# A two-layer decoder trunk: the last 512 columns of the first FFN's shift and scale move behind the layer norm

## The chip, the cores and the metric

The kernel runs on one core of one Trainium2 chip, as one program with one launch. The metric is the device time in microseconds (us); lower is better. A run of this kernel is quoted as the median of several executions. One execution was profiled by the hardware.

The core's engines run side by side and each takes its instructions in order. TensorE (PE, with its weight loads as PEld) multiplies matrices and writes to PSUM, of which this kernel uses eight banks. VectorE (DVE) and ScalarE (ACT) do element-wise work. GpSimd (POOL) does little here. SyncE (SP) issues the DMA loads.

## The reference

The input is one sequence of 256 positions with 2048 channels (`x`), and one conditioning vector `c` of 2048 numbers. There are two layers. Each has a token mixer and a gated FFN with a short convolution, and each of these is wrapped the same way:

```
c_act = silu(c)
for i in 0, 1:
    sh1, sc1, g1, sh2, sc2, g2 = split(c_act @ ada_w[i] + ada_b[i], 6)     # each 2048 long
    h = x * (1 + sc1) + sh1
    y = fox_attention(h)  (layer 0)   or   swa_attention(h)  (layer 1)
    x = layer_norm(alpha * x + (1 + g1) * y)
    h = x * (1 + sc2) + sh2
    u = causal depthwise conv of width 3 over positions of (h @ w_up)      # 2 * 5632 columns
    y = (silu(u[:5632]) * u[5632:]) @ w_down
    x = layer_norm(alpha * x + (1 + g2) * y)
```

All weights are 32-bit floats and stay in main memory until used. Layer 0's `w_up` is 2048 x 11264. `ada_w` is 2048 x 12288 for each layer, so 100 MB a layer for one vector times a matrix.

## The kernel before, in words

**Tiling.** The 2048 channels are 16 chunks of 128. Weights are streamed in blocks of two chunks by 512 columns (`stream`, L258): one DMA of 512 KB into a tile `w` (or, for the conditioning, `wa`) of a pool with ten buffers shared by all loads. Each block is split into a rounded high part `wh` (ScalarE, L266) and a residual `wl` (VectorE, L277), so that three fast matmul passes (high x high, low x high, high x low) give nearly full precision. The modulated activations are held as `hH` and `hL` in the same way. `w_mm` (L311) does one pair of chunks of a 512-column block with the weights stationary: 24 matmuls of 128x256. `x_mm` (L287) does it with the activations stationary: 12 matmuls of 128x512.

**Order.** `stream` does not run matmuls at once. It puts a function for each pair of chunks into the list `work`, and `settle` (L223) runs them two pairs behind. Just before a pair runs, `rest` (L229) issues the VectorE residuals for it and the next two pairs. A function added with `alone=True` (the set `lone`) is not looked past: no residual of a later pair is issued before it has run. The layer norm's function `between` (L1116) is added like that. Each pair calls `run_post` (one step of each deferred evacuation), then the matmuls, then one entry of `feeds` (modulation of two further chunks), then `tick`.

**Conditioning.** `tick` (L357) calls `ada_tick` (L463), which adds `ada["rate"]` to a debt and takes one step of the conditioning generator for each whole unit. `ada_list` (L365) gives the order of the vectors (layer, index): shift and scale of the FFN are 3 and 4, the gates 2 and 5, the mixer's shift and scale 0 and 1. A vector takes 32 steps of one load and one VectorE multiply-add into `acc` (L395, one 128x1024 piece for each of 16 chunks and two halves). A shift or scale vector (a column) is then summed over partitions: four groups of four transposes on TensorE (L433), four ScalarE activations each with a running sum into `tot` (L437), one VectorE addition of the bias (L419). A gate (a row) starts with a bias load by GpSimd and ends with four matmuls and activations (L405 to L407). After vector 4 the generator holds (`ada["held"]`, L442) until the norm has used it. `ada_need` (L469) takes steps until a given vector is there. `rate` is set by stage: 1.6 in the last part of the opening, 1.6, 1.6, 1.5 and 1.4 in the four FoX blocks (the first of these has no pair left by then), 1.3 in layer 0's output projection, 0.64 in its FFN's up-projection, 0.78 in its down-projection, 0.3 and 0.9 in layer 1's attention, 0.4 in its FFN.

**The norm and the FFN.** `residual` (L611) adds the output projection to `x` and gathers statistics. `between` asks for shift and scale in full, merges them with the norm's gain and bias into `G` and `B` (`merged`, L666), and calls `modulate` (L506): eight feeds, each two chunks. A feed normalises 512 columns of `x` where needed (L637 on ScalarE, L639 on VectorE), transposes four 128x128 blocks (L484), and writes `hH` and `hL` (L494 to L496 for the first two pairs, L498, L499, L84 and L85 for the others). Two feeds are run at once, and each further one after a pair of matmuls. `affine` (L650) applies the norm's gain and bias to `x` itself: 16 VectorE instructions (L657, L658) in eight later steps, with four loaded tiles.

`conv_ffn` (L1049) has two parts of 6 and 5 blocks. Each block has a gate column block and a value column block of `w_up` (512 columns each, eight pairs of chunks, two PSUM banks), so part one has 12 column blocks, 96 pairs. `evac` (L1063) takes a finished column block through the convolution, one 128x256 tile every two steps (ScalarE L1056, VectorE L1057 and L1059), then SiLU (L1075) or the gating product (L1080, L84, L85). Then comes the down-projection of that part, which needs gate (0,5).

The program's lists fix the order in which the work is written. A scheduler then places each instruction on its engine; it may move one ahead of others where its inputs and buffers are free, except those marked with `pin`, which keep their order.

Of the kernel before, what the change touches and what calls it, by code (L numbers as in the profile page):

```python
# [17 lines left out]
P = 128  # L18
# [23 lines left out]
def hybrid_trunk(ctx: ExitStack, tc: tile.TileContext, a: dict, out: bass.AP):  # L42
# [13 lines left out]
    def wtile(name="w"):  # L56
        return wp.tile([P, 2, WB], F32, tag="w", name=name)
# [310 lines left out]
    held = []  # L368
    HELD = {}

    def ada_vector(l, v):
        row = v % 3 == 2
        if (l, v) in HELD and HELD[l, v]:
            q = [cst.tile([P, 512], F32, tag=f"ha{i}", name="ha") for i in range(4)]
            part = lambda c, n: q[c // 512][:, c % 512:c % 512 + n]
            step_ = 512
        else:
            acc = cst.tile([P, D], F32, tag="acc", name="acc")
            part = lambda c, n: acc[:, c:c + n]
            step_ = D // 2  # L380
        if row:

            nc.gpsimd.dma_start(acc, a["ada_b"][l, v * D:(v + 1) * D].partition_broadcast(P))
            yield
            yield
        for k in range(KC):
            for c in range(0, D, D // 2):
                w = wtile("wa").rearrange("p a f -> p (a f)")
                pin(nc.sync.dma_start(w, a["ada_w"][l, k * P:(k + 1) * P, v * D + c:v * D + c + D // 2]), False)
                for o in range(0, D // 2, step_):  # L390
                    ac, wo = part(c + o, step_), w[:, o:o + step_]
                    if k == 0 and not row:
                        pin(nc.vector.tensor_scalar_mul(ac, wo, cact[:, 0:1]), True)
                    else:
                        pin(nc.vector.scalar_tensor_tensor(ac, wo, (cactp if row else cact)[:, k:k + 1], ac,  # L395
                                                           op0=ALU.mult, op1=ALU.add), True)
                yield
        if row:
            while not ada["gate_free"]:
                yield  # L400
            ada["gate_free"] = False
            g = cst.tile([P, D], F32, tag="gate", name="gate")
            for j in range(D // 512):
                ps = bank()
                mm(ps, onep, acc[:, j * 512:(j + 1) * 512], start=True, stop=True)  # L405
                yield
                nc.scalar.activation(g[:, j * 512:(j + 1) * 512], ps, AF.Copy, bias=1.0)  # L407
            gates[l, v] = g
            return
        ps = []  # L410

        def sums():
            ps.append(bank())
            for k in range(KC):
                pin(mm(ps[0][:, k:k + 1], part(k * P, P), ones[:, 0:1], start=True, stop=True))

        def finish():
            cv = cst.tile([P, KC], F32, tag=f"cv{v}", name="cv")
            pin(nc.vector.scalar_tensor_tensor(cv, ps[0][:, :KC], 1.0 if v % 3 else 0.0,  # L419
                                               acol[:, l, v * KC:(v + 1) * KC], op0=ALU.add, op1=ALU.add), True)  # L420
            cols[l, v] = cv

        if (l, v) in HELD:
            held.append((sums, finish))
            ada["held"] = not HELD[l, v]
            ready_cols.add((l, v))
        else:

            tot = sp.tile([P, KC], F32, tag="tot", bufs=1, name="tot")
            for k in range(0, KC, 4):  # L430
                tb = bank()
                for j in range(4):
                    nc.tensor.transpose(tb[:, j * P:(j + 1) * P], part((k + j) * P, P), ident)  # L433
                yield
                for j in range(4):
                    o = tb[:, j * P:(j + 1) * P]
                    nc.scalar.activation(o, o, AF.Identity, accum_out=tot[:, k + j:k + j + 1])  # L437
            yield
            ps.append(tot)
            finish()  # L440

            ada["held"] = v == 4  # L442

    ready_cols = set()

    def release():

        for s_, _ in held:
            s_()
        for _, f_ in held:  # L450
            f_()
        held.clear()
        ada["held"] = False

    def ada_step():
        if ada["gen"] is None:
# [10 lines left out]
            ada_step()  # L467

    def ada_need(l, v):  # L469
        while (l, v) not in cols and (l, v) not in gates and (l, v) not in ready_cols:  # L470
            ada_step()


# [29 lines left out]
    def hstat(kc, t):  # L503
        return hH[:, kc, t * P:(t + 1) * P], hL[:, kc, t * P:(t + 1) * P]

    def modulate(G, B, norm):  # L506
# [6 lines left out]
        feeds.extend([lambda k=k: feed(k) for k in range(0, KC, 2)])  # L513
        for _ in range(2):
            feeds.pop(0)()

    def opening(plan, proj, prep):

# [48 lines left out]
        for s_, todo in enumerate(todos):  # L567
            n = len(todo)
            if s_ == len(widths):
                then(lambda: ada.update(rate=1.6))  # L570
                for it in todo:
                    proj(*it)
                break
# [92 lines left out]
    def merged(l, v, lng, lnb, ll):  # L666

        sh, sc = cols[l, v], cols[l, v + 1]
        G = sp.tile([P, KC], F32, tag="G", name="G")
        B = sp.tile([P, KC], F32, tag="B", name="B")  # L670
        nc.vector.tensor_tensor(G, sc, lcol[:, lng, ll, :], op=ALU.mult)
        nc.vector.tensor_tensor(B, sc, lcol[:, lnb, ll, :], op=ALU.mult)
        nc.vector.tensor_tensor(B, B, sh, op=ALU.add)
        return G, B


# [50 lines left out]
    def out_proj(oT, full, w_o, l):  # L727
        def stat(kc, t):
            while kc not in full:
                step()  # L730
            return oT[kc][0][:, t * P:(t + 1) * P], oT[kc][1][:, t * P:(t + 1) * P]

        ps = {d: x_banks() for d in range(2)}

        def part(d, ks):
            use = x_mm_end(ps[d], stat, KC, 2) if d == D // WB - 1 else                 lambda kc, h, l_: x_mm(ps[d], kc, h, l_, stat, KC - 1)
            stream(w_o, 0, d * WB, ks, use)

        for i, ks in enumerate((range(0, 8), range(8, 12))):
            then(lambda i=i: ada.update(rate=((1.3, 1.3, 1.3, 1.3), (0.9,) * 4)[l][i]))  # L740
            for d in range(2):
                part(d, list(ks))
        then(lambda: ada_need(l, 2))
        for d in range(D // WB):
            if d < 2:
                part(d, list(range(12, KC)))
            else:
                then(lambda d=d: ada.update(rate=((1.3, 1.3, 1.3, 1.3), (0.9,) * 4)[l][d]))
# [300 lines left out]
    def conv_ffn(l):  # L1049
# [10 lines left out]
                                           op0=ALU.mult, op1=ALU.add)  # L1060
            return u

        def evac(ps, f0, then):  # L1063
            u = None
            for f in range(5):
                v = conv(ps[f // 2][:, f % 2, :], f0 + f) if f < 4 else None
                if u is not None:
                    then(f - 1, u)
                u = v
                yield  # L1070
                yield

        def silu(sil):
            def f_(f, u):
# [11 lines left out]
        sbs = [(0, 6), (6, NB)]  # L1086
        for si, (b0, b1) in enumerate(sbs):
            gT = []
            then(lambda: ada.update(rate=(0.64, 0.4)[l]))
            for b in range(b0, b1):  # L1090
                ps = w_stationary(w_up, b * WB)
                sil = [ttile("sil") for _ in range(2)]
                then(lambda ps=ps, b=b, sil=sil: defer(evac(ps, b * 4, silu(sil))))
                ps = w_stationary(w_up, DFF + b * WB)
                then(lambda ps=ps, b=b, sil=sil, gT=gT: defer(evac(ps, DFF // P + b * 4, gated(sil, gT))))

            def stat(kc, t, gT=gT):
                while kc >= len(gT):
# [3 lines left out]
            def ready(si=si):  # L1102
                if si == 0:
                    drain()
                ada_need(l, 5)
                ada["rate"] = (0.78, 0.4)[l]

            then(ready)
            for d in range(D // WB):
# [6 lines left out]
    def between(l, v, g, b, name, ll):  # L1116

        ada_need(l, v)
        ada_need(l, v + 1)
        release()  # L1120
        modulate(*merged(l, v, g, b, ll), normalise)
        behind[0] = 2
        later([affine(name, ll)])

    for l in range(DEPTH):
        if l > 0:
# [42 lines left out]
```

## Time and profile before

| | us |
|---|---|
| median of 3 runs | 2259.64 |
| lowest and highest | 2258.59, 2263.47 |
| the profiled execution | 2253.72 |
| its span, first to last instruction | 2251.9 |

In the profile's page, the first lines give the busy time of each engine. The digits after them divide the span into 40 equal slices (56 us each) and give the busy share in tenths. "Stretches" are rows of busy time by engine between two times. "Waits" rows say who waited for whom, then the total in us, how often, and the longest. "Groups" rows give line, engine, operation, what is written from what, shapes, how many, then busy us, mean ns of one, and idle time before them with what ended it. "Timeline" rows give start, duration and instruction in order of time.

The mean granted TensorE clock is 0.993. Layer 0's attention fills the time to about 360 us, its output projection the time to 465 us. The norm's first transposes stand at 470.52 us and the FFN's first matmul at 473.01 us.

### The profile page before, as it was taken

The numbers are of one execution on the slowest core, as the hardware profiler recorded it, in microseconds if no ns is written. First come the engines' busy times: TensorE is split into PE (matmuls) and PEld (weight loads), VectorE is DVE, ScalarE is ACT, GpSimd is POOL, SyncE is SP. The second block draws the span as 40 slices with busy tenths as digits, with TensorE's granted clock in tenths as the row PEclk, the third lists the DMA queues.
The fourth block names the chain that finished last, engine by engine and source line by source line (L and its number), as shares of the span: only waits on it lengthen the run. The fifth ranks groups of instructions, "written<-read, shape, count | busy, mean of one in ns | idle before, by whom it ended". The sixth has DMA issues, their size and how long they took to land. (4 is left out here: it accounts for less than half of the span.)

```text
span 2251.9 us, 38292 instructions
## 1 busy us (share of the span) xinstructions
PE 2197.1 (98%) x14853; PEld 2017.8 (90%) x14853; DVE 1794.3 (80%) x2450; ACT 1175.0 (52%) x1897; POOL 22.8 (1%) x53
## 2 busy tenths in 40 slices
PE   6999999999999999999999999999999999999997
PEld 6999888889999888999987788889999888999986
DVE  6989999979978968788788989779787555666756
ACT  3445656555555443655634588755555533454532
POOL 0000000000000000000000000000000000000000
PEclk9999999999999999999999999999999999999999
DMA  9999999969979989789897767658887566666663
GB/s 339 381 360 365 361 345 323 329 202 339 324 240 310 322 285 337 249 302 309 265 313 282 256 231 251 215 162 303 264 265 257 177 193 194 188 188 189 190 193 112
DMA packets 274248, 602.99 MB, mean 268 GB/s; under 512 B 21063, under 2 KB 29961, under 8 KB 273553
## 3 DMA queue, kind: packets, MB, share of 16 engines
q1 hardware_dynamic: 273008, 595.85, 79.3%
q0 software_dynamic: 1056, 4.69, 0.6%
q8 instruction: 116, 1.90, 0.3%
q14 instruction: 68, 0.55, 0.1%
HBM read 598.37 MB, written 2.10 MB: 267 GB/s over the span
## 5 line engine op out<-in xcount | busy, mean ns | idle before, releaser
L266 ACT CAST wh<-w 128x1024 fp32r<-128x1024 f32 x728 | 764.1, 1051 | 836.0 <-PE ws L75 304.6
L277 DVE TENSOR_TENSOR wl<-w,wh 128x1024 fp32r<-128x1024 f32 x728 | 888.1, 1223 | 352.6 <-ACT wh L266 331.8
L75 PE MATMUL ws<-hH,wh 128*128 128x256 f32 x3328 | 935.2, 282 | 4.9 <-ACT hH L84 2.1
L75 PE MATMUL ws<-hH,wl 128*128 128x256 f32 x3328 | 929.7, 281 | 3.2 <-DVE wl L277 3.1
L75 PE MATMUL ws<-hL,wh 128*128 128x256 f32 x3328 | 931.2, 280 | 0.0
L75 PEld LDWEIGHTS ws<-hH,wh 128*128 128x128 f32 x3328 | 628.7, 189 | 9.4 <-ACT hH L84 2.3
L75 PEld LDWEIGHTS ws<-hL,wh 128*128 128x128 f32 x3328 | 629.9, 189 | 2.9 <-issue 1.9
L75 PEld LDWEIGHTS ws<-hH,wl 128*128 128x128 f32 x3328 | 628.0, 189 | 4.7 <-DVE wl L277 4.6
L75 PE MATMUL xs<-wh,gT 128*128 128x512 f32 x1408 | 435.9, 390 | 0.0
L75 PEld LDWEIGHTS xs<-wh,gT 128*128 128x128 f32 x1408 | 264.4, 188 | 54.8
L75 PE MATMUL xs<-wl,gT 128*128 128x512 f32 x704 | 274.1, 389 | 0.0
L395 DVE SCALAR_TENSOR_TENSOR acc<-wa,cact,acc 128x1024 f32<-128x1024 f32 x180 | 228.5, 1277 | 0.3 <-DMA wa<-in_ada_w_dram 0.3
L395 DVE SCALAR_TENSOR_TENSOR acc<-wa,cactp,acc 128x1024 f32<-128x1024 f32 x128 | 162.7, 1279 | 1.0 <-DMA acc<-in_ada_b_dram 1.0
L75 PEld LDWEIGHTS xs<-wl,gT 128*128 128x128 f32 x704 | 132.2, 188 | 27.0
L75 PE MATMUL xs<-wl,hH 128*128 128x512 f32 x352 | 141.0, 401 | 3.1 <-DVE wl L277 3.1
L75 PE MATMUL xs<-wh,hH 128*128 128x512 f32 x352 | 142.0, 409 | 0.3 <-ACT hH L494 0.3
L75 PE MATMUL xs<-wh,hL 128*128 128x512 f32 x352 | 138.7, 397 | 0.0
L1056 ACT ACTIVATE u<-ws,ccol 128x256 f32<-128x256 f32 x176 | 96.5, 561 | 57.6 <-PE ws L75 49.1
L75 PE MATMUL xs<-wh,oT 128*128 128x512 f32 x384 | 125.1, 395 | 0.1
L1057 DVE SCALAR_TENSOR_TENSOR u<-ws,ccol,u 128x255 f32<-128x255 f32 x176 | 82.9, 480 | 19.0 <-ACT u L1056 19.0
L75 PEld LDWEIGHTS xs<-wh,oT 128*128 128x128 f32 x384 | 72.1, 188 | 14.8 <-ACT oT L84 0.5
L1059 DVE SCALAR_TENSOR_TENSOR u<-ws,ccol,u 128x254 f32<-128x254 f32 x176 | 83.6, 480 | 2.1
(218 smaller groups left out, 1597.3 us busy)
## 6 DMA issues: line engine op xcount, KB each, us to landing
w<-in_ffn_w_up_dram SPq DMA_DIRECT2D x352, 512.0 KB, 4.6
wa<-in_ada_w_dram SPq DMA_DIRECT2D x320, 512.0 KB, 5.5
w<-in_ffn_w_down_dram SPq DMA_DIRECT2D x176, 512.0 KB, 5.0
w<-in_fox_w_in_dram SPq DMA_DIRECT2D x96, 512.0 KB, 7.2
wo<-in_ada_w_dram SPq DMA_DIRECT2D x48, 512.0 KB, 8.9
w<-in_swa_w_in_dram SPq DMA_DIRECT2D x40, 512.0 KB, 5.3
w<-in_fox_w_o_dram SPq DMA_DIRECT2D x32, 512.0 KB, 6.0
w<-in_swa_w_o_dram SPq DMA_DIRECT2D x32, 512.0 KB, 5.2
```

The source lines that it names most:

```text
L75: return nc.tensor.matmul(o, lhsT, rhs, start=start, stop=stop, **kw)
L266: pin(nc.scalar.copy(h, w), False)
L277: pin(nc.vector.tensor_tensor(l, w, f32(h), op=ALU.subtract), behind[0] > 0)
L395: pin(nc.vector.scalar_tensor_tensor(ac, wo, (cactp if row else cact)[:, k:k + 1], ac, op0=ALU.mult, op1=ALU.add), True)
L1056: nc.scalar.activation(u, pf, AF.Identity, bias=cw(CW, f), scale=cw(2, f))
L1057: nc.vector.scalar_tensor_tensor(u[:, 1:], pf[:, :S - 1], cw(1, f), u[:, 1:], op0=ALU.mult, op1=ALU.add)
L1059: nc.vector.scalar_tensor_tensor(u[:, 2:], pf[:, :S - 2], cw(0, f), u[:, 2:], op0=ALU.mult, op1=ALU.add)
```

## The change

The first FFN's shift (0,3) and scale (0,4) are split at column 1536 (`LC` = 12 of 16 chunks). Before the norm, the generator computes columns 0 to 1535 of each: for each chunk one 1024-column piece as before, and for each two chunks one load that carries 512 columns of both, with two narrower multiply-adds. A new entry `(0, "late")` stands behind (0,4) in `ada_list`. It loads, for each of the 16 chunks of rows, the last 512 columns of both vectors with one DMA, and does one 1024-wide multiply-add. Two groups of four transposes and two bias additions finish it.

The first three column blocks of that FFN (gate block 0, value block 0, gate block 1) run over chunks 0 to 11 first, 18 pairs with six PSUM banks held. Then a function added with `alone=True` takes whatever is left of the late vector, merges columns 12 to 15 of `G` and `B`, and runs the last two feeds. Then the three column blocks run over chunks 12 to 15, six pairs. Their evacuations go through one chain that takes one tile a pair (`slow=False`). `affine` is put off to this point. The old way of holding vectors (`HELD`, `release`), which was not used, is removed.

The rates change: 1.4 in the last part of the opening, 1.35, 1.3, 1.3 and 1.25 in the FoX blocks, 1.2 in layer 0's output projection, 1.5 during the 18 pairs, 0.5 after them in the first part of the FFN, 0.7 in its second part, 0.8 in its down-projections.

```diff
-    ada_list = [(0, 3), (0, 2), (0, 4), (0, 5), (1, 0), (1, 1), (1, 3), (1, 2), (1, 4), (1, 5)]
+    ada_list = [(0, 3), (0, 2), (0, 4), (0, "late"), (0, 5), (1, 0), (1, 1), (1, 3), (1, 2), (1, 4), (1, 5)]
...
+        n = LC * P if (l, v) in SPLIT else D
...
         for k in range(KC):
-            for c in range(0, D, D // 2):
...
+            for c in range(0, n, D // 2):
+                w = wtile("wa")
+                if c + D // 2 <= n:
+                    w = w.rearrange("p a f -> p (a f)")
+                    pin(nc.sync.dma_start(w, a["ada_w"][l, k * P:(k + 1) * P, v * D + c:v * D + c + D // 2]), False)
+                    mac(acc[:, c:c + D // 2], w, k)
+                elif k % 2 == 0:
+                    pin(nc.sync.dma_start(w, a["ada_w"][l, k * P:(k + 2) * P, v * D + c:v * D + n]
+                                          .rearrange("(k p) f -> p k f", p=P)), False)
+                    for j in range(2):
+                        mac(acc[:, c:n], w[:, j, :], k + j)
+                else:
+                    continue
                 yield
...
+    LATE, LC = "late", KC - 4
+    SPLIT = {(0, 3), (0, 4)}
+
+    def ada_late(l):
+
+        n = KC - LC
+        acc = cst.tile([P, D], F32, tag="acc", name="acc")[:, :2 * n * P].rearrange("p (v f) -> p v f", v=2)
+        for k in range(KC):
+            w = wtile("wa")
+            pin(nc.sync.dma_start(w, a["ada_w"][l, k * P:(k + 1) * P, 3 * D:5 * D]
+                                  .rearrange("p (v f) -> p v f", f=D)[:, :, LC * P:]), False)
+            if k == 0:
+                pin(nc.vector.tensor_scalar_mul(acc, w, cact[:, 0:1]), True)
+            else:
+                pin(nc.vector.scalar_tensor_tensor(acc, w, cact[:, k:k + 1], acc, op0=ALU.mult, op1=ALU.add), True)
+            yield
+        tot = yield from ada_sums([acc[:, v, k * P:(k + 1) * P] for v in range(2) for k in range(n)])
+        for i in range(2):
+            ada_column(cols[l, 3 + i], tot, l, 3 + i, LC, n, i * n)
+        cols[l, LATE] = tot
...
-        for blk, rate in zip((0, 2, 1, 3), (1.6, 1.6, 1.5, 1.4)):
+        for blk, rate in zip((0, 2, 1, 3), (1.35, 1.3, 1.3, 1.25)):
...
+                then(lambda: ada.update(rate=1.5))
+                for i in range(len(first)):
+                    some(i, range(LC))
+                then(lambda: (late[l](), ada.update(rate=0.5)), True)
+                for i in range(len(first)):
+                    some(i, range(LC, KC))
+                    then(lambda i=i: (done.append(i), i or defer(chain())))
...
+        if (l, v) in SPLIT:
+            GB = merged(l, v, g, b, ll, ks=slice(0, LC))
+            modulate(*GB, normalise, (0, LC))
+
+            def more():
+                ada_need(l, LATE)
+                merged(l, v, g, b, ll, GB, slice(LC, KC))
+                modulate(*GB, normalise, (LC, KC))
+                while feeds:
+                    feeds.pop(0)()
+                later([affine(name, ll)])
+
+            late[l] = more
```

`ada_sums` is the old transposing and summing code, and `ada_column` the old bias addition, both for a given range of columns. `chain` evacuates the three first blocks one after the other.

More of the change, by code (lines that the diff above doesn't have):

```diff
@@ L409, in ada_vector @@
             return
[L410 to L421, printed above, removed]
@@ L444, in hybrid_trunk, with ada_sums @@
[L444 to L453, printed above, removed]
+        tot = yield from ada_sums([acc[:, k * P:(k + 1) * P] for k in range(n // P)])
+        cv = cst.tile([P, KC], F32, tag=f"cv{v}", name="cv")
+        ada_column(cv, tot, l, v, 0, n // P)
+        cols[l, v] = cv
+        ada["held"] = v == 4
+    def ada_sums(blocks):
+        tot = sp.tile([P, KC], F32, tag="tot", bufs=1, name="tot")
+        for k in range(0, len(blocks), 4):
+            tb = bank()
+            for j in range(4):
+                nc.tensor.transpose(tb[:, j * P:(j + 1) * P], blocks[k + j], ident)
+            yield
+            for j in range(4):
+                o = tb[:, j * P:(j + 1) * P]
+                nc.scalar.activation(o, o, AF.Identity, accum_out=tot[:, k + j:k + j + 1])
+        yield
+        return tot
@@ L469, in ada_need @@
     def ada_need(l, v):
-        while (l, v) not in cols and (l, v) not in gates and (l, v) not in ready_cols:
+        while (l, v) not in cols and (l, v) not in gates:
             ada_step()
```

125 lines of the change are left out of this document (62 added, 63 removed).

## The prediction

> **What bounds the kernel now.** I read the page first, then the stretches by stage, then who waited for whom in the stage before the first layer norm, then the order of time at that norm. The page's totals and slices:
>
> ```profile
> span 2251.9 us, 38292 instructions
> ...
> PE 2197.1 (98%) x14853; PEld 2017.8 (90%) x14853; DVE 1794.3 (80%) x2450; ACT 1175.0 (52%) x1897; POOL 22.8 (1%) x53
> ...
> PE   6999999999999999999999999999999999999997
> ...
> DVE  6989999979978968788788989779787555666756
> ```
>
> TensorE sets the time, so only stretches where it stops can give or lose anything. The stages around the change, by stretches (us; then busy us of PE, PEld, DVE, ACT, POOL; granted clock; DMA share; GB/s):
>
> ```profile
> 182.00:255.00 73.00, 71.06 (x529) 66.14 (x530) 69.95 (x112) 47.02 (x93) 5.29 (x11) 1.00 0.99 348
> 255.00:320.00 65.00, 63.23 (x442) 58.50 (x441) 59.72 (x78) 36.26 (x76) 0.00 (x0) 1.00 0.98 351
> 320.00:360.00 40.00, 38.20 (x270) 34.14 (x269) 35.12 (x49) 21.25 (x40) 0.00 (x0) 1.00 0.94 339
> 360.00:465.00 105.00, 103.85 (x496) 86.09 (x495) 91.51 (x120) 55.34 (x115) 0.54 (x1) 1.00 0.92 326
> 465.00:480.00 15.00, 11.39 (x68) 9.98 (x67) 13.60 (x27) 9.33 (x14) 1.12 (x2) 0.89 0.09 27
> ...
> 530.00:580.00 50.00, 50.00 (x431) 50.00 (x430) 49.47 (x65) 26.81 (x37) 0.00 (x0) 1.00 0.99 357
> 580.00:743.00 163.00, 163.00 (x1378) 161.08 (x1378) 138.86 (x177) 86.88 (x122) 0.00 (x0) 1.00 0.86 286
> ```
>
> From 182 to 465 us (FoX blocks and output projection) VectorE is busy 69.95 + 59.72 + 35.12 + 91.51 = 256.3 of 283 us, 91%, and the DMA engines 92 to 99%. From 530 to 580 us the first FFN runs with VectorE full (49.47 of 50) and yet TensorE never stops. From 580 to 743 us VectorE has 163 − 139 = 24 us free. What TensorE and its weight loads wait for between 182 and 465 us:
>
> ```profile
> PE xs L75 <- DVE wl L277: 2.6, 3, 1.8
> PE ws L75 <- DVE wl L277: 2.2, 4, 0.8
> PE sm L433 <- DVE acc L395: 1.4, 2, 1.1
> PE ws L75 <- ACT wh L266: 0.7, 1, 0.7
> ```
>
> ```profile
> PEld xs L75 <- DVE wl L277: 3.9, 4, 2.2
> PEld ws L75 <- DVE wl L277: 3.3, 5, 1.0
> ...
> PEld ws L75 <- ACT wh L266: 1.1, 1, 1.1
> ```
>
> Ends of matmuls are modelled, so I take the weight loads' account where there is one: 3.9 + 3.3 for late residuals `wl`, 1.1 for a late `wh`, and 1.4 for the shift-and-scale accumulator `acc`: 9.7 us. That is all that lighter VectorE and DMA work before the norm can give back.
>
> **The change, part by part.** Loads first. Before, vectors (0,3) and (0,4) have 32 loads of 512 KB each; after, 24 each, and 16 late loads carry the last 512 columns of both. 64 either way: no byte is saved, 16 loads (8.4 MB) move past the norm. VectorE's share, with the rows for 1024 and 512 columns (the second row is another instruction of the same operation, standing in for the new narrow one):
>
> ```profile
> L395 DVE SCALAR_TENSOR_TENSOR acc<-wa,cact,acc 128x1024 f32<-128x1024 f32 x56 | 70.2, 1275 | 0.0
> ```
>
> ```profile
> L277 DVE TENSOR_TENSOR wl<-w,wh 128x1024 fp32r<-128x1024 f32 x38 | 46.5, 1226 | 0.3 <-ACT wh L266 0.3
> L395 DVE SCALAR_TENSOR_TENSOR acc<-wa,cactp,acc 128x1024 f32<-128x1024 f32 x21 | 26.8, 1287 | 0.0
> L1057 DVE SCALAR_TENSOR_TENSOR u<-ws,ccol,u 128x255 f32<-128x255 f32 x15 | 7.3, 488 | 0.5 <-ACT u L1056 0.5
> ...
> L658 DVE SCALAR_TENSOR_TENSOR x<-ln,x 128x512 f32<-128x512 f32 x8 | 5.5, 693 | 0.0
> ```
>
> A split vector costs 16 × 1.28 + 16 × 0.69 = 31.5 us in place of 32 × 1.28 = 41.0, so two of them take 19 us from VectorE before the norm; late, 16 × 1.28 = 20.5 us come back.
>
> *Gain before the norm.* VectorE goes from 256.3 to 237 of 283 us, 91% to 84%; DMA falls by 8.4 of some 96 MB (283 us at about 338 GB/s), 9%. The lower rates spread this: 1.6 to 1.3 in the block from 182 us takes 0.3 × 1.28 = 0.4 us from each pair of chunks, less in later ones. If waits go as load over free time, 0.91/0.09 becomes 0.84/0.16 and they halve: 9.7 × 0.48 = 4.7 us. If every one goes, 9.7. The accumulator's 1.4 us may stay, and both resources lighten together; I take **6.5 us**.
>
> Does the work still end before the norm? Counted in steps of the conditioning generator: before, 38 + 39 + 38 = 115, with 107.8 granted by the end of output columns 0 and 1 and 1.3 for each pair in column 2, so it ends in that column's sixth pair. After, 29 + 39 + 29 = 97, with 93.3 granted by then and 1.2 a pair: the fourth. The last column row of before lies 16.5 us ahead of the norm's closing matmuls, so no wait arises there:
>
> ```profile
> 445.78 0.17 DVE L419 SCALAR_TENSOR_TENSOR cv<-tot,acol 128x16 f32<-128x16 f32 x1
> ```
>
> *Start of the FFN.* The norm's own stop and the two fast pairs stay. One pair of chunks is 24 matmuls; 431 in 50 us make 0.116 us each, 2.78 us a pair. VectorE in order: `wl` 1.23, 1.5 × 1.28 for the late columns, and in the first four pairs also modulation (0.55 + 0.69); 4.4 us in those, 3.1 in the following seven: more than 2.78 in all eleven. Over a longer stretch the balance is:
>
> ```profile
> 473.00:580.00 107.00, 106.66 (x896) 106.25 (x897) 104.21 (x138) 58.94 (x81) 0.00 (x0) 0.98 0.88 302
> ```
>
> Here TensorE does 36 pairs (38 residuals, made two pairs ahead) and VectorE is busy 104.2 of 107 us. By pair 36 the new rates grant 18 × 1.5 + 18 × 0.5 = 36 steps; 20 go to the late generator (16 loads, 2 transposes, 2 ends), leaving 16, of which 14 are multiply-adds of (0,5): 30 in place of 21. In a run of them they start 1.2 us apart:
>
> ```profile
> 497.44 1.28 DVE L395 SCALAR_TENSOR_TENSOR acc<-wa,cactp,acc 128x1024 f32<-128x1024 f32 x1
> 498.63 0.69 DVE L658 SCALAR_TENSOR_TENSOR x<-ln,x 128x512 f32<-128x512 f32 x1
> ```
>
> Nine more are 10.8 us; the affine of `x` comes later but still inside; the first three columns' evacuation comes late and then one tile a pair, 14 tiles by then in place of 15, −1 us. Demand is 114 us against 107: 7 us too much. Residuals are issued two pairs ahead, so VectorE may be up to 2 × 2.78 = 5.6 us behind without stopping TensorE: the cost is 1.4 us with that whole lead, 7 with none.
>
> *The new boundary at chunk 12.* The two feeds are popped at once after pair 18. If their transposes stay there in TensorE's order, it waits for transposes, activation, cast and residual:
>
> ```profile
> 470.52 0.66 PE L484 MATMUL sm<-ident,x 128*128 128x128 f32 x4 [2.43 <-ACT x L637]
> 472.03 0.66 PE L484 MATMUL sm<-ident,x 128*128 128x128 f32 x4 [0.85 <-DVE x L639]
> 473.01 0.54 PE L75 MATMUL ws<-hH,wh 128*128 128x256 f32 x2 [0.33 <-ACT hH L494]
> ...
> 494.83 0.56 ACT L498 ACTIVATE t<-sm,B,G 128x256 f32<-128x256 f32 x1
> 495.42 0.62 ACT L84 CAST hH<-t 128x512 fp32r<-128x512 f32 x1
> ```
>
> 0.66 + 0.56 + 0.62 + about 0.5 for hand-overs is 2.3 us; if they are ordered earlier, behind the matmuls of chunks 0 to 11, nothing. The normalising itself already runs ahead of need. The late sums are there in time: 20 steps at 1.5 take 13.3 of 18 pairs. During such a stop VectorE catches up, so it is not added in full to the overload: together I take **5 us**, bounds 1.4 (lead whole, transposes early) and 7 + 3.9 = 10.9.
>
> The 3.9 holds a clock loss: the stretch 465 to 480 us around the norm's stop has clock 0.89, 15 × 0.11 = 1.6 us, on top of 2.3. The Trainium skill ("TensorE: Matmul & The Clock Gate", Part 1) has the clock fall to half only after an idle window of about 3.4 us. The norm's three stops above sum to 3.6 us and its clock does drop, which agrees; by that rule a 2.3 us stop should cost no clock, and the upper bound would be 9.3.
>
> *Other queues.* Late loads enter SyncE's queue among the up-projection's: 13 + 16 loads, 15.2 MB, for eleven pairs (11 × 2.78 + 4 × 0.66 = 33 us with the transposes). The pool's ten buffers fill while DMA is idle around the norm (share 0.09); the other 19, 10 MB, need 302 GB/s, and 357 was moved from 530 to 580 us: nothing. Without that cover 15.2/0.357 = 43 us, 10 late, in the same pairs as VectorE's overload. On GpSimd's queue the bias load of (0,5) now waits for the late transposes; that queue is 1% busy. Later rates: by the end of the first FFN 172 steps are granted to (0,5) and on, in place of 181 (18 × 1.5 + 78 × 0.5 + 48 × 0.8 + 80 × 0.7 + 40 × 0.8 − 20, against 96 × 0.64 + 48 × 0.78 + 80 × 0.64 + 40 × 0.78). Layer 1's last column, at 0.9 a pair, then comes ten pairs (27 us) later. It has 38.6 us of room:
>
> ```profile
> 1456.82 0.17 DVE L419 SCALAR_TENSOR_TENSOR cv<-tot,acol 128x16 f32<-128x16 f32 x1
> ```
>
> ```profile
> 1495.40 0.55 PE L484 MATMUL sm<-ident,x 128*128 128x128 f32 x3 [2.43 <-ACT x L637]
> ```
>
> Nothing, therefore, while that room holds; each step too late would cost 1.28 us.
>
> *Sum:* −6.5 + 5 = −1.5 us. The profiled execution took 2253.72 us (span 2251.9), 5.9 under the median of the three runs, 2259.64; so 2252.2 for an execution like it and **2258** for the median. A measurement here tells about 0.2%, 4.5 us, from no change.
>
> **Rivals.**
>
> 1. *VectorE has room enough.* The FFN start costs 1.4 us, since the lead absorbs the overload as it does from 530 to 580 us, and 8 us of waits vanish: −6.6, **2253**. For it: TensorE at 50.00 with VectorE at 49.47. Against: there VectorE's demand does not exceed its time.
> 2. *The bound moves to VectorE behind the norm* (slower). The place is pairs 4 to 18. The norm leaves no lead, since no residual past it is made before it, so TensorE waits for `wl` from the point where 4.4 us of work meet 2.78 + 0.66 us of matmuls and transposes; then it stops at chunk 12. 10.9 − 4.7 = +6.2, **2266**. Against: at 476 us of before three residuals were soon done.
> 3. *The waits before the norm come from the order of work on VectorE, not its load*; then 2 us go and 5 come: +3, **2263**, no change that can be told.
> 4. *It doesn't do what it says*: the late sums are not ready at pair 18. Each missing step then costs 1.28 us with TensorE stopped; five of them, 6.4 us more: 2264.5. Against: 4.7 pairs, 13 us, of margin.
>
> **How the numbers follow.** The balanced forecast has 0.38, the first rival 0.33 (0.31 for clear gains, 0.02 for gains too small to tell), the second 0.18, the third 0.06, the fourth 0.05. Same is the forecast, the third and that 0.02: 0.46; faster 0.31; slower 0.23 (the second and the fourth). The low end takes all 9.7 us and no cost behind the norm, 2250; the high end is the second rival, 2266. The forecast's own range is 2255 to 2262, its gain or cost off by 3 us.
>
> **What would show it.** Right: `wl` waits between 182 us and the norm fall from 7.2 to about 3 us, the norm comes some 6 us earlier, and the 18 pairs behind it take longer than 18 × 2.78 us plus the norm's start, with VectorE full and TensorE waiting on `wl` or, at chunk 12, on `hH` or transposes. Wrong: no such waits behind the norm (first rival), the norm at the same time (third), or TensorE waiting on `acc` at pair 18 (fourth). A wait on layer 1's column near 1490 us would break the last part.

## The result and the profile after

| | before | after |
|---|---|---|
| median of four runs, us | 2259.85 (2258.59 to 2263.47) | 2271.86 (2270.66 to 2273.69) |
| the profiled execution, us | 2253.72 | 2270.66 |
| its span, us | 2251.9 | 2268.9 |

The ratio is 1.0051, 95% interval 1.0034 to 1.0069: the change makes the kernel 12 us slower. That lies outside the range given. The two profiled executions differ by 17 us, since that of before was 6 us under its median and that of after 1 us under.

The stages, from the profiled executions. A stage begins with the first matmul that reads its operands, for instance the down-projection with the first one on `gT`:

| stage, us | before | after | difference |
|---|---|---|---|
| up to the FFN's first matmul | 473.0 | 466.3 | −6.7 |
| first FFN, up-projection, part one | 277.5 | 295.3 | +17.8 |
| its down-projection | 132.5 | 132.5 | 0.0 |
| up-projection, part two | 227.0 | 225.8 | −1.2 |
| down-projection and norm | 114.5 | 116.0 | +1.5 |
| layer 1's attention | 151.8 | 155.0 | +3.2 |
| layer 1's output projection and norm | 121.5 | 123.9 | +2.4 |
| layer 1's FFN to the last matmul | 740.2 | 740.2 | 0.0 |

The ends of the second row stand in the timeline of TensorE, kernel after:

```profile
466.29 0.58 PE L75 MATMUL ws<-hH,wh 128*128 128x256 f32 x1
...
761.61 0.40 PE L75 MATMUL xs<-wh,gT 128*128 128x512 f32 x1
```

So the gain before the norm is there, 17.8 us are lost behind it, and 5.6 more in layer 1's attention and output projection. First the gain. Kernel after, 182 us to the last output projection, first as a stretch, then the waits of the weight loads, then the waits of the matmuls:

```profile
182.00:459.00 277.00, 274.49 (x1734) 245.29 (x1733) 242.36 (x357) 159.99 (x308) 5.31 (x11) 1.00 0.90 314
```

```profile
PEld sm L429 <- ACT wh L266: 2.9, 1, 2.9
```

```profile
PE sm L429 <- DVE acc L386: 2.4, 1, 2.4
```

No wait for `wl` is left in this stretch, where before had 7.2 us. VectorE is busy 242.4 of 277 us in place of 256.3 of 283. TensorE's one stop is again for an accumulator, at 240 us; the two rows are that same stop, seen from the weight loads and from the matmuls. Before had 1.4 us of such waits, in two stops.

Now the loss. Kernel after, stretches behind the norm, and what TensorE waits for from 466 to 600 us:

```profile
466.00:505.00 39.00, 38.11 (x306) 37.43 (x304) 36.39 (x43) 15.97 (x23) 0.00 (x0) 0.95 0.83 283
505.00:517.00 12.00, 5.77 (x38) 5.59 (x38) 8.17 (x12) 6.08 (x20) 0.60 (x1) 0.72 1.04 398
517.00:530.00 13.00, 13.00 (x114) 13.00 (x113) 8.91 (x8) 4.92 (x5) 0.00 (x0) 1.00 0.78 254
530.00:537.00 7.00, 3.77 (x22) 2.89 (x21) 6.26 (x8) 2.85 (x5) 0.00 (x0) 0.85 1.02 369
```

```profile
PE sm L429 <- DVE acc L455: 6.2, 1, 6.2
PE sm L491 <- DVE t L506: 2.6, 1, 2.6
PE ws L75 <- DVE hL L85: 0.9, 2, 0.5
PE ws L75 <- ACT wh L266: 0.6, 1, 0.6
PE ws L75 <- DVE wl L277: 0.5, 1, 0.5
```

There are two places. At 505 us TensorE stops for 6.2 us. The clock of 0.72 is a mean over 12 us that include this stop; cut finer, it is 0.69 in the stop and 0.50 in the 3.0 us behind it, in which TensorE works again:

```profile
505.20:511.40 6.20, 0.02 (x1) 0.00 (x0) 6.20 (x7) 2.83 (x3) 0.00 (x0) 0.69 1.04 397
511.40:514.40 3.00, 2.94 (x14) 2.98 (x15) 1.10 (x2) 1.75 (x11) 0.60 (x1) 0.50 1.03 402
```

At 530 us, the boundary at chunk 12, it stops again and the clock is 0.85 over 7 us. The residuals `wl`, which the prediction expected as the wait, account for 0.5 us. The timelines of TensorE and VectorE around 505 us show what stands where:

```profile
504.94 0.28 PE L75 MATMUL ws<-hH,wl 128*128 128x256 f32 x1
511.45 0.88 PE L429 MATMUL sm<-ident,acc 128*128 128x128 f32 x3 [6.23 <-DVE acc L455]
```

```profile
506.56 1.22 DVE L277 TENSOR_TENSOR wl<-w,wh 128x1024 fp32r<-128x1024 f32 x1
507.70 1.28 DVE L455 SCALAR_TENSOR_TENSOR acc<-wa,cact,acc 128x1024 f32<-128x1024 f32 x1
508.90 1.22 DVE L277 TENSOR_TENSOR wl<-w,wh 128x1024 fp32r<-128x1024 f32 x1
510.03 1.28 DVE L455 SCALAR_TENSOR_TENSOR acc<-wa,cact,acc 128x1024 f32<-128x1024 f32 x1
```

The next instruction in TensorE's queue at 505 us is a transpose of the late accumulator. VectorE finishes the last multiply-add of that accumulator only at 511.3 us. Meanwhile it makes one residual after the other (those at 506.56 and 508.90 are seen here) for matmuls that stand behind the transposes. TensorE didn't pass over the waiting transpose. That matmuls behind it could have run is what the first experiment tests.

At the boundary, VectorE's row `t`, which the second stop waits for, stands behind a multiply-add of the gate (0,5):

```profile
532.84 1.28 DVE L386 SCALAR_TENSOR_TENSOR acc<-wa,cactp,acc 128x1024 f32<-128x1024 f32 x1
534.04 0.54 DVE L506 TENSOR_SCALAR t<-sm,G,B 128x256 f32<-128x256 f32 x1
```

### The profile page after: what moved, and what is told of

The parts are those of the page before. It is cut to its first block, busy times and chain, and to the rows that moved or that the text cites. A ratio compares the mean times of both kernels' runs of the same rounds, so it can differ in the third digit from the quotient of the medians.

```text
span 2268.9 us, 38315 instructions
## 1 busy us (share of the span) xinstructions
PE 2205.0 (97%) x14853; PEld 2023.6 (89%) x14853; DVE 1798.2 (79%) x2471; ACT 1176.8 (52%) x1897; POOL 22.0 (1%) x53
## 5 line engine op out<-in xcount | busy, mean ns | idle before, releaser
L386 DVE SCALAR_TENSOR_TENSOR acc<-wa,cact,acc 128x1024 f32<-128x1024 f32 (+1 forms) x180 | 212.6, 1188 | 0.2
```

## The experiments

Two theories stood against each other for the stop at 505 us. The *order* theory: the late transposes stand too early in TensorE's queue. The *load* theory: VectorE or DMA is behind in these pairs anyway, and if TensorE did not wait for `acc` it would wait for `wl` or `wh`. The ratios below are against the kernel before, run on the same chip; stages are from each run's profiled execution.

| run | median us (before beside it) | ratio, 95% interval | FFN starts at | part one | layer 1, attention and output |
|---|---|---|---|---|---|
| before | 2259.85 | | 473.0 | 277.5 | 273.3 |
| after | 2271.86 (2259.85) | 1.0051, 1.0034 to 1.0069 | 466.3 | 295.3 | 278.9 |
| sums later | 2261.34 (2257.97) | 1.0017, 1.0004 to 1.0030 | 464.7 | 284.7 | 278.5 |
| gate held | 2269.35 (2257.97) | 1.0053, 1.0033 to 1.0073 | 466.7 | 290.7 | 281.7 |
| one late load | 2275.10 (2257.97) | 1.0075, 1.0058 to 1.0091 | 468.5 | 296.3 | 281.8 |
| narrow multiply-adds | 2267.41 (2257.97) | 1.0040, 1.0028 to 1.0053 | 466.5 | 288.3 | 280.5 |
| reorder only | 2263.55 (2257.72) | 1.0029, 1.0016 to 1.0041 | 475.3 | 282.6 | 274.0 |
| before, later rates | 2263.49 (2257.72) | 1.0024, 1.0012 to 1.0036 | 475.1 | 276.9 | 279.9 |
| sums later and rates | 2259.24 (2257.72) | 1.0008, 0.9996 to 1.0021 | 470.2 | 284.2 | 275.2 |
| rate 1.2 | 2262.35 (2257.72) | 1.0015, 1.0005 to 1.0026 | 465.7 | 283.3 | 281.0 |
| tuned | 2258.89 (2257.89) | 1.0005, 0.9996 to 1.0013 | 467.6 | 284.3 | 276.0 |
| before, more rate | 2257.82 (2257.89) | 0.9998, 0.9989 to 1.0006 | 478.0 | 277.2 | 274.1 |
| reorder, affine slower | 2263.90 (2257.89) | 1.0022, 1.0010 to 1.0033 | 475.7 | 284.1 | 274.0 |

### Sums later

```diff
+        for _ in range(6):
+            yield
         tot = yield from ada_sums([acc[:, v, k * P:(k + 1) * P] for v in range(2) for k in range(n)])
```

> Edit: six empty steps of the generator between the last late multiply-add and the late transposes, so that TensorE meets these transposes about four pairs later. Order theory: the changed kernel's TensorE stops 6.4 us at the late transposes (and then runs at a lower granted clock for some 5 us) only because they stand ahead of matmuls that were ready; the stop goes, and the first part of the up-projection shrinks from 295.3 us by 8 to 10 us; whole kernel about 2262 to 2264 us. Load theory (rival): VectorE and the DMA engines are behind in these pairs anyway, so TensorE waits for wl or wh instead of acc; the part shrinks by less than 3 us, whole kernel 2269 or more. Both: (0,5) starts six steps later, so layer 1 may lose up to 2 us more.

Part one fell from 295.3 to 284.7 us, by 10.6. The kernel is 3.4 us slower than before on the same chip, where the kernel after was 12.0. What TensorE still waits for from 466 to 600 us in this run, and its first stretches:

```profile
PE ws L75 <- DVE hL L85: 0.9, 2, 0.5
PE ws L75 <- DVE wl L277: 0.9, 2, 0.6
PE sm L493 <- DVE t L508: 0.6, 1, 0.6
PE ws L75 <- ACT wh L266: 0.6, 1, 0.6
```

```profile
464.00:503.00 39.00, 37.77 (x306) 37.12 (x305) 36.32 (x44) 16.21 (x22) 0.00 (x0) 0.96 0.81 278
503.00:530.00 27.00, 25.84 (x214) 24.75 (x213) 20.57 (x25) 15.75 (x31) 0.60 (x1) 1.00 0.94 360
```

The stop did not come back as a wait for `wl` (0.9 us), and the clock stays at 1.00 from 503 to 530 us. The order theory holds; the load theory's 3 us at most is far off. The six empty steps also take multiply-adds of (0,5) out of VectorE's next pairs; the following run has that relief too, and the stop stays.

### Gate held until the boundary

```diff
         cols[l, LATE] = tot
+        ada["held"] = True
...
                 ada_need(l, LATE)
+                ada["held"] = False
```

> Edit: after the late vector the generator holds until the boundary at chunk 12, so no multiply-add of gate (0,5) stands in VectorE's queue ahead of the boundary's modulation. Queue theory: of the stop at the boundary (530 to 537 us) the 2.8 us on VectorE's t go, 3 to 4 us in all with the clock; the 6.4 us at the late transposes stay; whole kernel about 2268 us. Rival (the boundary's own chain of transposes, activation, cast and two free PSUM banks sets it): under 1.5 us gained, 2271 us.

The wait for `t` at the boundary fell from 2.6 to 0.6 us, and part one by 4.6 us, a little over the 3 to 4 expected. The stop at the late transposes stayed:

```profile
PE sm L429 <- DVE acc L455: 5.5, 1, 5.5
PE ws L75 <- DVE hL L85: 0.9, 2, 0.5
PE sm L492 <- DVE t L507: 0.6, 1, 0.6
```

Layer 1 took 2.8 us more, most of it because the gate's steps now come later still: its last column comes at 1510.01 us, in the norm, and the norm's stop is 5.0 us in place of 2.4.

```profile
PE sm L492 <- ACT x L646: 5.0, 1, 5.0
```

So the kernel is 11.4 us slower than before on the same chip, where the kernel after was 12.0: no gain that can be told, and the 3 to 4 us expected for the whole kernel did not come. In "sums later" the same wait is 0.6 as well: six empty steps also keep (0,5) from starting ahead of the boundary, so its 10.6 us hold this effect too.

### One late load, and narrow multiply-adds

These ask what makes the accumulator late. The first has one late load in place of 16, and every multiply-add reads it, so the late columns are made from the first chunk of rows alone. The second has all 16 loads but 15 multiply-adds of 2 × 8 columns, which leaves out nearly all of the late columns' sum.

```diff
-        for k in range(KC):
-            w = wtile("wa")
-            pin(nc.sync.dma_start(w, a["ada_w"][l, k * P:(k + 1) * P, 3 * D:5 * D]
+        w = wtile("wa")
+        pin(nc.sync.dma_start(w, a["ada_w"][l, 0:P, 3 * D:5 * D]
...
+        for k in range(KC):
```

```diff
-                pin(nc.vector.scalar_tensor_tensor(acc, w, cact[:, k:k + 1], acc, op0=ALU.mult, op1=ALU.add), True)
+                pin(nc.vector.scalar_tensor_tensor(acc[:, :, :8], w[:, :, :8], cact[:, k:k + 1], acc[:, :, :8],
+                                                   op0=ALU.mult, op1=ALU.add), True)
```

> Edit: one late load in place of 16; all 16 multiply-adds read that tile, so VectorE's work is whole and 15 loads (7.9 MB) are left out (the late columns are then computed from the first chunk's rows alone). If the late accumulator is late because of DMA: the 6.4 us stop goes, and the first part of the up-projection shrinks by 8 to 10 us. If it is late because of VectorE's own queue: the stop stays within 2 us of 6.4, and the part shrinks by less than 3 us.

> Edit: all 16 late loads, but 15 of the 16 multiply-adds work on 8 columns of each vector in place of 512, so DMA is whole and some 15 us of VectorE work are left out (with it nearly all of the late columns' sum). If the late accumulator is late because of VectorE's queue: the stop at the transposes goes and the first part of the up-projection shrinks by 8 to 10 us or more. If because of DMA: the stop stays at 4 us or more, and the part shrinks by less than 4 us.

With one load, the 39 us behind the norm as a stretch, and then the longest of TensorE's waits from 466 to 600 us:

```profile
468.00:507.00 39.00, 37.38 (x302) 36.76 (x301) 37.90 (x44) 18.05 (x24) 0.00 (x0) 0.96 0.55 162
```

```profile
PE sm L429 <- DVE acc L455: 5.8, 1, 5.8
```

The DMA engines are little more than half busy, 0.55 against 0.83, and the stop is still 5.8 us; part one is even 1 us longer. VectorE is busy 37.9 of 39 us. With narrow multiply-adds there is no wait for `acc` at all, but 3.2 us for `wl`:

```profile
PE ws L75 <- DVE wl L277: 3.2, 6, 1.1
PE sm L492 <- DVE t L507: 0.7, 1, 0.7
PE ws L75 <- ACT wh L266: 0.6, 1, 0.6
```

Part one took 288.3 us, 7 less, where 8 to 10 were expected. So it is VectorE's queue that makes the accumulator late, not DMA. The waits for `wl` come at 536 to 581 us, behind the boundary, and the clock is 0.51 from 525 to 528.5 us, right behind the boundary's stop. Why `wl` is late there, and so why this run is not as short as "sums later", was not tested.

### Rate 1.2

```diff
-                then(lambda: ada.update(rate=1.5))
+                then(lambda: ada.update(rate=1.2))
```

> Edit: the rate during the 18 pairs is 1.2 in place of 1.5, so a pair holds 1.23 + 1.2 x 1.28 = 2.8 us of VectorE work (2.6 start to start) against 2.78 us of matmuls: no overload after the modulated pairs, and the late transposes come about three pairs later in the program. If VectorE's overload makes the accumulator late: the stop of 6.4 us falls under 1.5 us, and the first part of the up-projection takes 283 to 286 us. If a stop of over 4 us stays, the overload is not the cause. Layer 1 as in the changed kernel or up to 3 us slower, since 5 steps fewer are granted.

The wait for `acc` is 1.1 us, and part one 283.3 us:

```profile
PE ws L75 <- DVE wl L277: 1.2, 2, 0.9
PE sm L429 <- DVE acc L455: 1.1, 1, 1.1
PE sm L491 <- DVE t L506: 0.6, 1, 0.6
```

One number alone removes 12 us of part one. It does two things at once, less work for VectorE in each pair and transposes some three pairs later, so it doesn't tell the one from the other. With 5 steps fewer granted, layer 1 took 281.0 us, 2 more than in the kernel after.

### Reorder only, and its affine slower

The FFN begins with three column blocks over chunks 0 to 11, but shift and scale are computed in full before the norm, at the rates of before. The second run also spreads the affine of `x`.

```diff
-    ada_list = [(0, 3), (0, 2), (0, 4), (0, "late"), (0, 5), (1, 0), ...
+    ada_list = [(0, 3), (0, 2), (0, 4), (0, 5), (1, 0), ...
-        n = LC * P if (l, v) in SPLIT else D
+        n = D
...
-                then(lambda: ada.update(rate=1.5))
+                then(lambda: ada.update(rate=0.64))
-                then(lambda: (late[l](), ada.update(rate=0.5)), True)
+                then(lambda: late[l](), True)
...
-                ada_need(l, LATE)
```

```diff
-                later([affine(name, ll)])
+                later([affine(name, ll)], 2)
```

> Edit: shift and scale are computed in full before the norm, at the rates of the kernel before, and nothing is late; only the order of the FFN's start is changed (three column blocks over chunks 0 to 11, the boundary, then chunks 12 to 15). It prices the reorder alone. If the boundary and the postponed evacuation cost something by themselves: the first part of the up-projection takes 281 to 284 us against 277.5 before, whole kernel +4 to +6 us. If they cost only because late work stands in VectorE's queue: 279 us or less, within 2 us of before. The time to the first norm should equal before's (FFN start at 473 us) in both.

> Edit: the reorder alone, with the affine of x behind the boundary at half its pace (one piece every second pair). If the reorder's 5 us are mostly VectorE's load behind the boundary (affine and three evacuations at one tile a pair): the waits for wl 80 to 120 us behind the FFN's start (about 3.4 us) fall to under 1.5 us, and the first part of the up-projection takes 279.5 to 281 us in place of 282.6. If the reorder's price is the boundary itself: 282 to 283 us.

The reorder by itself takes 5.1 us in part one and about as much in the whole kernel (1.0029). TensorE's waits in part one, first the reorder alone, then the kernel before in the same stage, then the reorder with the slower affine:

```profile
PE ws L75 <- DVE wl L277: 1.9, 2, 1.2
PE sm L491 <- DVE t L506: 0.7, 1, 0.7
```

```profile
PE ws L75 <- DVE wl L277: 0.3, 1, 0.3
```

```profile
PE ws L75 <- DVE wl L277: 3.1, 3, 1.4
```

The slower affine did not do what was expected of it: the waits for `wl` don't go, they come some 10 us later and grow from 1.9 to 3.1. Measured by the start of each matmul against a steady 0.116 us, the reorder loses some 2 us more than before around the boundary and 3.0 us between 60 and 120 us behind the FFN's start, where before loses 0.2; with the slower affine, 4.2 us there. Which of the works that now meet behind the boundary (affine, three evacuations at one tile a pair, the gate) would have to go was not tried one by one, and stays open.

### Before, with later rates and with more rate

```diff
-            then(lambda: ada.update(rate=(0.64, 0.4)[l]))
+            then(lambda si=si: ada.update(rate=((0.5, 0.7)[si], 0.4)[l]))
...
-                ada["rate"] = (0.78, 0.4)[l]
+                ada["rate"] = (0.8, 0.4)[l]
```

The second run has 0.66 and 0.8 in the same two places.

> Edit of the kernel before: only the rates behind the first norm are those of the changed kernel (0.5 and 0.7 in the up-projections, 0.8 in the down-projections), so 174 steps in place of 181 are granted by the end of the first FFN. If the later conditioning is what makes layer 1 slower: its attention and output projection take 4 to 5.6 us more than the 273.3 us of before, and the whole kernel is 3 to 6 us slower. If the layer 1 loss has another cause (the order of the scheduler): under 1.5 us more.

> Edit of the kernel before: 0.66 in layer 0's up-projections in place of 0.64 and 0.8 in its down-projections in place of 0.78, so 185 steps in place of 181 by the end of the first FFN. If a step moved out of layer 1's attention is worth about 0.7 us (7 steps cost 5.7 us in the run with fewer): 2 to 3 us faster than before. If layer 1 loses only when the steps pass a certain point: within 1 us of before.

The rates of the changed kernel, put into the kernel before and nothing else, make layer 1's attention and output projection 6.6 us longer (279.9) and the whole kernel slower by 1.0024. Groups of VectorE in that stage, kernel before and then kernel after:

```profile
L395 DVE SCALAR_TENSOR_TENSOR acc<-wa,cact,acc 128x1024 f32<-128x1024 f32 x30 | 38.3, 1275 | 0.0
L395 DVE SCALAR_TENSOR_TENSOR acc<-wa,cactp,acc 128x1024 f32<-128x1024 f32 x6 | 7.7, 1280 | 0.0
```

```profile
L386 DVE SCALAR_TENSOR_TENSOR acc<-wa,cact,acc 128x1024 f32<-128x1024 f32 x30 | 38.1, 1273 | 0.0
L386 DVE SCALAR_TENSOR_TENSOR acc<-wa,cactp,acc 128x1024 f32<-128x1024 f32 x14 | 17.9, 1276 | 0.0
```

Eight more multiply-adds fall into it, 46 in place of 38 with the two that start a vector. More rate did not give the opposite: 0.9998, layer 1 at 274.1 us with 33 of them. So layer 1 loses when steps are pushed into its attention, but pulling five more out brings nothing. All thirteen profiles fit this: with 33 to 38 multiply-adds in that stage it takes 273.3 to 276.0 us, with 45 to 53 it takes 278.5 to 281.8, and within the two groups more of them is not always longer. Half of the loss or more stands in TensorE's waits for weights in `x_mm`. Kernel after, then before with later rates; in the kernel before no matmul there waits for `wl` or `wh`:

```profile
PE xs L75 <- DVE wl L277: 2.9, 2, 1.8
```

```profile
PE xs L75 <- ACT wh L266: 2.8, 2, 1.4
PE xs L75 <- DVE wl L277: 1.1, 2, 0.6
```

The rest is spread over smaller waits.

### Sums later and rates; tuned

The first keeps the six empty steps and raises the rates behind the boundary to 0.6 and 0.79, so that the 181 steps of before are granted. The second puts together what the runs above suggest: rate 1.25, two empty steps, half the pace for the affine, rates 0.6, 0.8 and 0.85.

```diff
-            then(lambda si=si: ada.update(rate=((0.5, 0.7)[si], 0.4)[l]))
+            then(lambda si=si: ada.update(rate=((0.6, 0.79)[si], 0.4)[l]))
...
-                then(lambda: (late[l](), ada.update(rate=0.5)), True)
+                then(lambda: (late[l](), ada.update(rate=0.6)), True)
```

> Edit: the six empty steps of the first experiment, and the rates after the boundary raised to 0.6 (first part) and 0.79 (second part), which restores the 181 steps by the end of the first FFN. If the rates explain layer 1: its attention and output projection fall from 278.5 to about 273.5 us, and the kernel comes to 2255 to 2257 us, 1 to 3 us under before. If not: they stay within 1.5 us of 278.5, and the kernel near 2261 us.

> Edit: the changed kernel with rate 1.25 during the 18 pairs, two empty steps ahead of the late transposes, the affine of x behind the boundary at half its pace, 0.6 behind the boundary, 0.8 in the second part and 0.85 in the down-projections (186 steps by the end of the first FFN, before 181). If the three causes found so far (place of the late transposes, steps in layer 1, load behind the boundary) are all of the loss: the first part of the up-projection takes 280 to 282 us, layer 1's attention and output projection about 272 us, the whole kernel 2252 to 2255 us, 3 to 5 us under before and clear of it. If the reorder costs its 5 us whatever is done: about 2257 us, no change that can be told.

Layer 1 came back to 275.2 and 276.0 us, short of the 273.5 and 272 expected, and both kernels are level with before (1.0008 and 1.0005, intervals across 1). None beats it, though 1 to 3 and 3 to 5 us were expected; for the second run part one took 284.3 us where 280 to 282 were expected, and its rival came nearer, that the reorder costs its 5 us whatever is done. With its two mistakes mended, the change gives before the norm about what it takes behind it: part one is 7 us longer than before in both.

## Why the prediction was wrong, point by point

*The gain before the norm was right.* The term was 6.5 us, the profile shows 6.7. A single profile can't carry that digit: the five profiles of kernels with the old order before the norm start the FFN between 473.0 and 478.0 us (mean 475.4), the eight with the new one between 464.7 and 470.2 (mean 467.0). The mean difference is 8.4 us, inside the bounds 4.7 to 9.7. The waits for `wl` went as named, though all of them and not half; the third rival is out. One price was off: the narrow multiply-add took 0.75 us and not 0.69, so VectorE was relieved of 17 us and not 19.

*The start of the FFN is the step that failed: the statement that the late sums "are there in time: 20 steps at 1.5 take 13.3 of 18 pairs".* It counted steps of the generator, which is a place in the program, and took 4.7 pairs of margin from pair 18. But TensorE meets the late transposes where the program puts them, around pair 12, and there VectorE was 6 us behind. The prediction itself had computed that VectorE needs 4.4 and then 3.1 us a pair against 2.78, and then let TensorE's two-pair lead absorb it. That lead covers residuals. It doesn't cover the accumulator, whose multiply-adds stand behind them in VectorE's queue and whose reader stands ahead of later matmuls in TensorE's. The price was 6.4 us between the two matmul starts (6.5 less one steady step) and the clock behind it, 3.0 us × 0.50 = 1.5 us: some 8 of the 10.6 that "sums later" gave back. Most of the rest is the boundary, where the wait for `t` was 2.0 us shorter in that run. The fourth rival named a wait on `acc`, but at pair 18, for missing steps, and with a chance of 0.05.

The prediction had the rule at hand and did not use it: the Trainium skill ("TensorE: Matmul & The Clock Gate", Part 2, Step-by-step) says that matmuls stay in program order and only weight loads are pulled ahead. The row at 511.45 us agrees: ready matmuls stood 6.2 us behind a waiting transpose.

*The rest of that term came out near in size, in part by luck.* Without the stop, part one is 284.7 − 277.5 = 7.2 us longer, where 5 was taken with bounds 1.4 to 10.9. The 5 were for nine more multiply-adds and for the stop at the boundary. But 5.1 of the 7.2 are the reorder alone, with no late work: some 2 around the boundary, as forecast, and 3.0 behind it, where the affine and the evacuations meet, which the forecast had at nothing and at −1 us. At the boundary of the kernel after, VectorE's `t` came 2.6 us late, since multiply-adds of (0,5) stood ahead of it ("gate held" takes them away, and 0.6 us are left); the prediction had counted on VectorE catching up there.

*The clock.* The kernel after and its seven variants with the split all stop once for 2.4 us at about 240 us, for the accumulator. In six of these eight profiles the clock stays at 1.00 behind that stop; in "one late load" and "sums later and rates" it falls to half. Their stretches behind it:

```profile
243.40:246.80 3.40, 3.40 (x12) 2.83 (x11) 2.88 (x4) 2.28 (x10) 0.00 (x0) 0.50 0.77 248
```

```profile
244.50:248.00 3.50, 3.18 (x11) 2.84 (x12) 2.82 (x4) 1.51 (x6) 0.00 (x0) 0.51 0.88 306
```

So a stop about as long as the 2.3 us that the forecast had at the boundary can cost 1.7 us of clock (3.4 us at half) or nothing; what decides is not shown. In "sums later" the boundary's stop of 0.6 us left the clock at 1.00. The forecast weighed its 1.6 us against the Trainium skill's window of about 3.4 us ("TensorE: Matmul & The Clock Gate", Part 1), by which such a stop costs no clock. Two of the eight profiles differ from that.

*DMA was right.* Its cost was put at nothing, and leaving out 15 of the 16 late loads shortened nothing.

*Layer 1 is the second step that failed.* The prediction counted nine steps fewer by the end of the first FFN, and priced them at nothing "while that room holds". The room did hold in the kernel after: the last column came at 1498.28 us, 14 us ahead of the norm's transposes. VectorE's timeline, kernel after:

```profile
1498.28 0.17 DVE L438 SCALAR_TENSOR_TENSOR cv<-tot,acol 128x16 f32<-128x16 f32 x1 [0.26 <-ACT sm L433]
```

But eight multiply-adds moved into that stage, and cost 5.6 us. A due time that is kept is not a cost of nothing. In three other runs the room did run out: in "sums later", "rate 1.2" and "gate held" the last column comes 0.7 to 1.4 us ahead of the norm's transposes, and the norm's stop is 3.2, 3.2 and 5.0 us in place of 2.4.

*The sum,* by the profiled executions: −6.7 before the norm; +10.6 for the place of the late transposes, with the gate's work ahead of the boundary; +7.2 for the reorder and the late load; +5.6 in layer 1; +0.3 in the rest. That is +17.0, as the spans have it; the medians differ by 12. The forecast was −6.5 + 5 + 0. The second rival, slower, had the sign and VectorE as the cause, but the wrong wait and half the size.

## What to carry to other kernels

When work is moved behind a point and cut into background steps, follow each of its instructions into each engine's queue: a consumer on the critical engine blocks all that is ready behind it, so put it there only after the producer's queue has really come so far, and not when the program's count says so. A lead that protects one kind of data does not protect another that stands behind it. And if a rate is lowered, look where the steps that are then missing will run: the stage that gets them may lose more than the one that is relieved gains.

## What was not expected of the hardware

In the profiled execution of "sums later and rates", layer 1's FFN took 747.0 us to its last matmul, where all other profiles have 739.5 to 741.5. From about 1530 to 1750 us the 128x256 matmuls started some 0.119 us after one another, not 0.116, at a granted clock of 1.00 and with nothing waited for. One stretch, kernel before and then this run:

```profile
1550.00:1600.00 50.00, 50.00 (x431) 50.00 (x430) 42.80 (x59) 27.38 (x38) 0.00 (x0) 1.00 0.88 298
```

```profile
1550.00:1600.00 50.00, 50.00 (x419) 50.00 (x418) 40.15 (x52) 25.38 (x35) 0.00 (x0) 1.00 0.87 290
```

419 matmuls in place of 431, 3% fewer. The time of this profiled execution was 2266.35 us, against a median of 2259.24 for the kernel: 7 us, which is what this stage would give. Whether others of its executions have the slow matmuls was not shown, since one was profiled, and what makes them slow is open. It limits what can be told of a kernel from few runs.
